# A hybrid decoder layer on one core: five first products, quartered first weights, and roots and reciprocals of norms on rows of tokens

## The chip, the cores and the metric

The kernel runs on one core of a Trainium2 chip. The engines of a core are named as in the profile: PE (matrix multiply, with PEld for its weight loads), DVE (vector), ACT (scalar functions), POOL (GpSimd) and SP, which issues most transfers. Each engine works through its own list of instructions in a fixed order. The metric is the device time of one execution in microseconds (us); lower is better.

## The reference, cut to what matters

One layer for a prompt of 1,024 tokens and 8 groups of 8 sample tokens, 1,088 in all, with 1,024 features, all in f32.

```python
def rmsnorm(x, g):
    y = x * rsqrt(mean(x * x, axis=-1, keepdims=True) + EPS)
    return y * g

xn = rmsnorm(x, norm1_g)
q, k, v, glu_a, glu_b, gate_a, gate_b = split(xn @ w_in)
branch_a = attend(q, k, v, mask, sinks) @ w_o_attn       # window 128, 16 heads, 4 kv heads
u = glu_a * sigmoid(glu_b)
c = dwconv(u)                                            # 31 taps
branch_b = silu(layernorm(c)) @ w_pb
h = x + (sigmoid(gate_a) * branch_a + sigmoid(gate_b) * branch_b) @ w_out
up = dwconv(rmsnorm(h, norm2_g) @ w_up)                  # 3 taps, 2 x 2816 channels
gate, val = split(up)
y = rmsnorm(h + (silu(gate) * val) @ w_down, norm_f_g)
```

A norm's factor belongs to a token (a column of the transposed tokens), so `xn @ w` is `(x * g) @ w` times that factor, and the factor may be applied to the product.

## The kernel before, in words

Features lie on the 128 partitions, in `KT` = 8 blocks, and tokens on the columns, in three chunks of 384, 384 and 320. Products must be as exact as f32, but PE takes fp32r operands, so each operand is split into a high part (a copy rounded to fp32r, on ACT) and a low part (the remainder, on DVE), and `mm3` makes three matmuls of each pair: high with high (L179), weight high with token low (L180), weight low with token high (L181). A product of one weight (1,024 by 128, 512 KB) with one chunk has 8 x 3 = 24 matmuls and goes into one of eight PSUM banks, four of the tag `mm` and four of the tag `aux`. `weight` loads weights two ahead through SP, and `w_split` casts them (L157, ACT) and makes the remainder (L158, DVE).

**The opening** (`phase_x`). The weights of `w_in` come in the order of `SEQUENCE`: b, a, q0, g, q0, and so on. The first four (`FIRST`) are run chunk by chunk on tokens that have been multiplied by g1 but not yet normed: `norm1_raw` makes their high and low parts (L217, L218). Meanwhile `norm1_stats` squares the tokens (L227, ACT), adds the squares of two blocks (L229, DVE) and lets PE multiply the four sums by a constant matrix 1/1024 (L233), which adds up over the partitions and gives each partition the mean square of each token. `rstd` then takes root and reciprocal of the whole 128 x 384 tile (L248 ACT, L249 DVE). The evacuations of the first four products multiply by this tile (`ev_b` L719, `ev_a` L725, `ev_q` L732, the gate L610). `norm1` then writes the normed tokens over the un-normed ones: a multiply on DVE (L242), the high part on ACT (L243), the low part half on DVE and half on POOL (L245). From the fifth weight on (the second q0), products run on normed tokens.

SP's list in the opening is: weight 0, the eight blocks of chunk 0, weights 1 and 2, chunk 1 in eight pieces, weight 3, chunk 2, then a weight at a time. ACT's own queue carries the constants, all in one transfer, ahead of a first small root that makes ACT load its table (L517). DVE derives four small constant tiles (L519 to L528) before it does anything else. PE first runs twelve matmuls on the constant matrix (L531).

**After the opening.** While PE streams the remaining products of `w_in`, attention units are woven in: scores, softmax (L265 on DVE, L270 to L272), turned by PE (L303), split into `pth` and `ptl` (`split_ps`, L196 on ACT and L197 on DVE) and multiplied with v (L315, L316). The convolution of 31 taps runs on DVE as a long list of multiply-adds (L417), which the order puts between all else.

**The end.** `ffn_down` runs the last products over three chunks of 352, 352 and 256 tokens and keeps the last 128 tokens for `tail`. For each of the three chunks `final` multiplies the sum of squares by the constant matrix (one f32 matmul, L1228), takes root and reciprocal of the whole tile (L248, L249) and scales the output in eight steps on DVE (L1232). `tail` computes the last tokens with tokens on the partitions: two products of 512 columns, their squares summed on ACT (L1252), then a short chain (L1254 to L1256) and the scaling (L1259).

The order on each engine is made ahead of time by a scheduler that follows priorities (the order of the code, moved back by `later`) and estimated costs; an edit in one place may move instructions elsewhere.

Of the kernel before, what the change touches and what calls it, by code (L numbers as in the profile page):

```python
# [45 lines left out]
FIRST = 4  # L46
# [20 lines left out]
W_SECOND = 3  # L67
W_PARTS = 2
# [8 lines left out]
def weight_order():  # L77
# [25 lines left out]
    ("ident", P),  # L103
    ("g1", KT), ("g2", KT), ("gf", KT), ("lng", KT), ("lnb", KT),
    ("cw", KT * CW), ("cb", KT), ("sink", 16), ("srow", 2), ("eps", 1),
# [10 lines left out]
class Build:  # L116
# [21 lines left out]
    def w_load(self):  # L138
        i = len(self.w_raw)
        if i < len(self.order):  # L140
            r = self.t(*(lambda p, x: (p, [P, DM], x))(*self.raw_slot(i)), bufs=2)
            self.nc.sync.dma_start(r, self.a["wall"][i])
            self.w_raw.append(r)

    def w_split(self):
        i = len(self.w_hl)
        if i < len(self.order):
            r = self.w_raw[i]
            pool, x = self.slot(i)
# [4 lines left out]
            m = W_PARTS if i < FIRST else 1  # L154
            for x in range(m):
                z = slice(x * DM // m, (x + 1) * DM // m)
                self.nc.scalar.copy(h[:, z], r[:, z])  # L157
                self.nc.vector.tensor_tensor(l[:, z], r[:, z], h[:, z].bitcast(F32), ALU.subtract)  # L158
            self.w_hl.append((h, l))
# [3 lines left out]

    def raw_slot(self, i):
        return self.wp, "wraw"
# [28 lines left out]

    def split_ps(self, h, l, src):
        self.nc.scalar.copy(h, src)  # L196
        self.nc.vector.tensor_tensor(l, src, h.bitcast(F32), ALU.subtract)  # L197
# [9 lines left out]
    def norm1_load(self, pp, c):  # L207
        o, n = CHUNKS[c]
        xr = self.t(pp, [P, KT, n], f"xr{c}")
        for k in range(KT):  # L210
            self.nc.sync.dma_start(xr[:, k, :], self.a["xT"][k, :, o:o + n])
        return xr

    def norm1_raw(self, c, xr, xh, xl):
        for k in range(KT):
            h = xh[c][:, k, :]
# [4 lines left out]
    def norm1_stats(self, pp, c, xr):  # L221
        nc = self.nc
        n = CHUNKS[c][1]
        ps = self.bank("aux")
        for k in range(KT):
            sq = self.t(pp, [P, 384], "sq", bufs=SQ_BUFS)
            nc.scalar.activation(sq[:, :n], xr[:, k, :], AF.Square)  # L227
            if k % FOLD:
                nc.vector.tensor_tensor(sq[:, :n], sq[:, :n], last[:, :n], ALU.add)  # L229
            last = sq  # L230
            if k % FOLD == FOLD - 1:
                with self.later(MEAN_LATER[c]):
                    nc.tensor.matmul(ps[:, :n], self.mean, sq[:, :n], start=k == FOLD - 1, stop=k == KT - 1)  # L233
        rstd = self.t(pp, [P, 384], f"rstd{c}")
        self.rstd(rstd[:, :n], ps[:, :n])
        return rstd

# [9 lines left out]
    def rstd(self, out, var):  # L247
        self.nc.scalar.activation(out, var, AF.Sqrt, bias=self.c("eps", 0))  # L248
# [245 lines left out]
    def run(self):  # L494
        nc, tc, a = self.nc, self.tc, self.a
        es = ExitStack()
        with es:
# [13 lines left out]
            nc.scalar.dma_start(self.consts, a["consts"])  # L511
# [7 lines left out]
            nc.vector.tensor_scalar(self.nsink, self.c("sink", 0, 16), -1.0, None, ALU.mult)  # L519
            self.cb2 = self.t(g, [P, KT], "cb2")  # L520
            nc.vector.tensor_scalar(self.cb2, self.c("cb", 0, KT), 2.0, None, ALU.mult)
            self.hsum = self.t(g, [P, KT * 16], "hsum")
            w = self.c("cw", 0, KT * CW).rearrange("p (i k) -> p i k", i=KT)
            hv = self.hsum.rearrange("p (i k) -> p i k", i=KT)
            nc.vector.tensor_tensor(hv[:, :, 0:15], w[:, :, 0:30:2], w[:, :, 1:31:2], ALU.add)
            nc.vector.tensor_copy(hv[:, :, 15:16], w[:, :, 30:31])
            self.nsrow = self.t(g, [P, 2], "nsrow")
            nc.vector.tensor_scalar(self.nsrow, self.c("srow", 0, 2), -1.0, None, ALU.mult)  # L528
# [4 lines left out]
            self.phase_x()  # L533

# [3 lines left out]
    def phase_x(self):  # L538
# [161 lines left out]
        self.slot = lambda i: (p0, "xyz"[i - 2]) if 2 <= i < FIRST else (self.wp, i % 2)  # L700
        for _ in range(W_FIRST):
            self.w_load()
        xr = [self.norm1_load(p0, 0)]
        while len(self.w_raw) < W_SECOND:
            self.w_load()
# [8 lines left out]
        def ev_b(c, o, n, ps):  # L714
            for d, x, y, r in u_part(u, o, n):
                if self.scale is None:
# [679 lines left out]
```

## Time and profile before

| | us |
|---|---|
| runs (3): median, lowest to highest | 1704.49, 1704.23 to 1704.73 |
| profiled execution | 1704.84 |
| its span, from first to last instruction | 1703.1 |
| PE busy in it | 1681.4 |
| DVE busy in it | 1287.1 |
| ACT busy in it | 848.6 |

The profile's page gives busy times of the engines, the chain of waits that ended last, and groups of equal instructions. A table of windows gives, for each stretch of time, the busy time of PE, PEld, DVE, ACT and POOL (with the number of instructions), the clock that PE was granted (1.00 is full), the busy share of the DMA engines and GB/s. A row of the timeline begins with start and duration; in brackets behind it stands how long the engine had been idle, and what it had waited for. The times are those of one execution. Matmul durations overlap: in a stream the distance between two starts tells what one costs.

### The profile page before, as it was taken

Reading aid. Unit: us, or ns where it says so; the run is one execution under the profiler, and the core shown is the slowest. Engines: PE = TensorE matmul, PEld = TensorE weight load, DVE = VectorE, ACT = ScalarE, POOL = GpSimd, SP = SyncE. Lnnn points to the kernel's source line nnn. Section 1 sums busy time; section 2 is a strip of 40 time slices with the busy share of each in tenths; the row PEclk is TensorE's granted clock in tenths of the full one; section 3 lists DMA queues with packets and bytes.
Section 4 is the critical chain, followed back from the end, with each engine's and each line's share of the span. In section 5 each row is a group of like instructions: output and inputs, shape, how many; then the busy total and the mean of one; then the engine's idle time right before and its main releaser. Section 6 shows DMA issues by size and latency. Waiting matters only on the chain.

```text
span 1703.1 us, 29147 instructions
## 1 busy us (share of the span) xinstructions
PE 1681.4 (99%) x11390; PEld 1660.6 (98%) x11390; DVE 1287.1 (76%) x2236; ACT 848.6 (50%) x1718; POOL 244.5 (14%) x430
## 2 busy tenths in 40 slices
PE   9999999999999999999999999999999999999998
PEld 8899999999999999999999999999999999999997
DVE  8999989999679986855546977777777773754437
ACT  7524477733588746973233544444444455311102
POOL 1300112130011211100000341222222220000000
PEclk9999999999999999999999999999999999999999
DMA  5112123232211265553344232222222323853103
GB/s 195 50 54 69 63 74 98 69 133 57 82 44 51 76 238 163 171 167 125 122 130 139 58 124 77 77 77 77 77 77 77 90 66 125 268 143 102 52 1 106
DMA packets 103466, 172.16 MB, mean 101 GB/s; under 512 B 44400, under 2 KB 69376, under 8 KB 103312
## 3 DMA queue, kind: packets, MB, share of 16 engines
q1 hardware_dynamic: 89760, 124.92, 24.8%
q0 software_dynamic: 13424, 45.15, 7.3%
q8 instruction: 89, 1.46, 0.4%
q14 instruction: 49, 0.40, 0.1%
q10 hardware_dynamic: 144, 0.23, 0.0%
HBM read 124.74 MB, written 47.50 MB: 101 GB/s over the span
## 4 chain that ended last, share of the span: by engine, by line
PE 89%; DVE 7%; ACT 2%; issue 1%; DMA 0%; POOL 0%; DVEq 0%; ACTq 0%; POOLq 0%
PE mm L180 22%; PE mm L181 21%; PE mm L179 21%; PE aux L181 6%; PE aux L180 6%; PE aux L179 6%; DVE c L417 2%; PE aux L303 1%; DVE bt L417 1%; PE aux L315 1%; PE aux L316 1%; PE aux L293 1%; PE aux L294 1%; ACT p L270 0%; PE aux L356 0%
## 5 line engine op out<-in xcount | busy, mean ns | idle before, releaser
L179 PE MATMUL mm<-xh,whi 128*128 128x384 f32 (+1 forms) x944 | 314.7, 333 | 0.1
L180 PE MATMUL mm<-xl,whi 128*128 128x384 f32 (+1 forms) x944 | 309.6, 328 | 3.2 <-DVE xl L245 1.7
L181 PE MATMUL mm<-xh,wlo 128*128 128x384 f32 (+1 forms) x944 | 308.8, 327 | 0.0
L180 PEld LDWEIGHTS mm<-xl,whi 128*128 128x128 f32 x944 | 178.0, 189 | 6.7 <-DVE xl L245 2.8
L179 PEld LDWEIGHTS mm<-xh,whi 128*128 128x128 f32 x944 | 178.1, 189 | 1.3 <-ACT xh L217 0.4
L181 PEld LDWEIGHTS mm<-xh,wlo 128*128 128x128 f32 x944 | 177.8, 188 | 0.1
L157 ACT CAST whi<-wraw 128x1024 fp32r<-128x1024 f32 (+1 forms) x88 | 90.4, 1030 | 175.3 <-PE aux L180 81.2
L158 DVE TENSOR_TENSOR wlo<-wraw,whi 128x1024 fp32r<-128x1024 f32 (+1 forms) x88 | 104.9, 1196 | 42.1 <-ACT whi L157 41.6
L1006 DVE SCALAR_TENSOR_TENSOR acc<-st,fc,acc 128x1104 f32<-128x1104 f32 x88 | 119.7, 1363 | 4.4 <-ACT acc L1004 3.6
L179 PE MATMUL mm<-mh,whi 128*128 128x272 f32 x368 | 106.6, 290 | 0.0
L180 PE MATMUL mm<-ml,whi 128*128 128x272 f32 x368 | 106.1, 288 | 0.0
L181 PE MATMUL mm<-mh,wlo 128*128 128x272 f32 x360 | 104.1, 289 | 0.0
L417 DVE SCALAR_TENSOR_TENSOR bt<-u,consts,bt 128x513 f32<-128x513 f32 x120 | 89.7, 747 | 0.6
L417 DVE SCALAR_TENSOR_TENSOR c<-sm,hsum,c 128x512 f32<-128x512 f32 x120 | 89.5, 746 | 0.6
L417 DVE SCALAR_TENSOR_TENSOR c<-u,consts,c 128x512 f32<-128x512 f32 x112 | 83.4, 745 | 0.5
L179 PE MATMUL mm<-gh,whi 128*128 128x384 f32 (+3 forms) x240 | 78.0, 325 | 3.4 <-ACT gh L196 3.4
L180 PE MATMUL mm<-gll,whi 128*128 128x384 f32 (+3 forms) x240 | 78.5, 327 | 0.7 <-DVE gll L197 0.7
L181 PE MATMUL mm<-gh,wlo 128*128 128x384 f32 (+3 forms) x240 | 78.7, 328 | 0.0
L180 PE MATMUL aux<-gll,whi 128*128 128x384 f32 (+3 forms) x240 | 78.2, 326 | 0.0
L179 PE MATMUL aux<-gh,whi 128*128 128x384 f32 (+3 forms) x240 | 78.2, 326 | 0.0
L181 PE MATMUL aux<-gh,wlo 128*128 128x384 f32 (+3 forms) x240 | 78.2, 326 | 0.0
L179 PE MATMUL mm<-th,whi 128*128 128x272 f32 x240 | 70.1, 292 | 2.4 <-ACT st L1128 2.2
(380 smaller groups left out, 5252.1 us busy)
## 6 DMA issues: line engine op xcount, KB each, us to landing
wraw<-wall SPq DMA_DIRECT2D x134, 512.0 KB, 4.1
d_g<-acc POOLq DMA_DIRECT2D x22, 552.0 KB, 5.2
gr<-d_g SPq DMA_DIRECT2D x20, 512.0 KB, 5.0
ga<-d_ga SPq DMA_DIRECT2D x8, 544.0 KB, 4.1
gb<-d_gb SPq DMA_DIRECT2D x8, 544.0 KB, 3.7
mar<-d_ma SPq DMA_DIRECT2D x8, 544.0 KB, 5.5
xr<-xT SPq DMA_DIRECT2D x32, 136.0 KB, 2.6
d_h<-H POOLq DMA_DIRECT2D x4, 1088.0 KB, 5.8
```

The costliest lines, as they stand in the source:

```text
L157: self.nc.scalar.copy(h[:, z], r[:, z])
L158: self.nc.vector.tensor_tensor(l[:, z], r[:, z], h[:, z].bitcast(F32), ALU.subtract)
L179: mm(ps, wh, xh, start=first, stop=False, skip_group_check=more)
L180: mm(ps, wh, xl, start=False, stop=False, skip_group_check=more)
L181: mm(ps, wl, xh, start=False, stop=last, skip_group_check=more)
L293: nc.tensor.matmul(ps[:, j, :], q[g][:, h, qs], kd[g][:, keys], start=True, stop=False)
L294: nc.tensor.matmul(ps[:, j, :], q[g][:, h, qs], kl[g][:, keys], start=False, stop=True)
L303: nc.tensor.transpose(ps[:, h * P:(h + 1) * P], pt[:, h, kb * P:(kb + 1) * P], self.ident)
L315: nc.tensor.matmul(av, v, ph, start=kb == kbs[0], stop=False)
L316: nc.tensor.matmul(av, v, pl, start=False, stop=kb == kbs[-1])
L417: mac = lambda o, x, w: nc.vector.scalar_tensor_tensor(o, x, w, o, ALU.mult, ALU.add)
L1006: nc.vector.scalar_tensor_tensor(acc, st[:, k:k + AW], fw(f, k), acc, ALU.mult, ALU.add)
```

## The change

Five things are edited.

- `FIRST` goes from 4 to 5: the second q0 product also runs on un-normed tokens and is scaled in its evacuation (`ev_q(j)`). Its split weight lies in columns of the tiles `q` that are not yet used (`spare`); the third weight is loaded into a tile of the convolution.
- The first two weights are loaded and split in quarters, between the blocks of chunk 0: SP's list is now x0, x1, a quarter of each weight, x2, x3, and so on, and only the first two quarters go through ACT's queue. For chunk 0 the first two products run side by side (`stream_side`): each block of tokens is used for both before the next. Chunks 1 and 2 come in four transfers each instead of eight.
- The constants come in two transfers, g1 and eps first; the derived tiles are made after the streams of chunk 0 (`derive`).
- `norm1_stats` adds the squares of all eight blocks on DVE, 7 adds instead of 4, and `rstd_rows` takes the place of the four mean matmuls: for each piece of at most 128 tokens (`PIECES`: 3 for 384, 4 for 320 and 352, 2 for 256) one f32 matmul with the squares as weights and one column of 1/1024, which puts the tokens on partitions (L270); a root and a reciprocal of a tile of a few columns (L287, L288); for each piece one f32 matmul that broadcasts the row with the identity (L273); and a copy on ACT (L275).
- `final` uses `rstd_rows` too.

```diff
-FIRST = 4
+FIRST = 5
...
-RAW = (0, 1, 2)
-W_FIRST = 1
-FIRST_TAGS = (("mm", "mm", "mm", "mm"), ("aux", "aux", "mm", "mm"), ("mm", "mm", "aux", "aux"))
-FOLD = 2
+FIRST_TAGS = (("mm", "mm", "mm", "mm", "aux"), ("aux", "mm", "mm", "mm", "mm"), ("aux", "mm", "mm", "mm", "mm"))
...
-W_PARTS = 2
+W_PARTS = 4
+PIECES = {384: 3, 320: 4, 352: 4, 256: 2}
...
+    def w_parts(self, m):
...
+        def part(x):
+            z = slice(x * DM // m, (x + 1) * DM // m)
+            self.nc.scalar.copy(h[:, z], r[:, z])
+            self.nc.vector.tensor_tensor(l[:, z], r[:, z], h[:, z].bitcast(F32), ALU.subtract)
+        return [lambda x=x: part(x) for x in range(m)]
...
+    def stream_side(self, xs, evacs, ws, tags, c):
+        o, n = CHUNKS[c]
+        ps = [self.bank(tag) for tag in tags]
+        for k in range(KT):
+            self.tick()
+            ks = slice(k * P, (k + 1) * P)
+            xh, xl = xs(c, k)
+            for p, (wh, wl) in zip(ps, ws):
+                self.mm3(p[:, :n], wh[:, ks], wl[:, ks], xh, xl, k == 0, k == KT - 1)
+        for p, evac in zip(ps, evacs):
+            evac(c, o, n, p)
...
+        for k in range(0, KT, 2):
+            if c == 0:
+                z = slice(k * P, (k + 2) * P)
+                for i, w in enumerate(self.w_raw):
+                    (self.nc.sync if k else self.nc.scalar).dma_start(w[:, z], self.a["wall"][i][:, z])
+                for j in (k, k + 1):
+                    self.nc.sync.dma_start(xr[:, j, :], self.a["xT"][j, :, o:o + n])
+            else:
+                self.nc.sync.dma_start(xr[:, k:k + 2, :], self.a["xT"][k:k + 2, :, o:o + n].rearrange("k p t -> p k t"))
...
-            if k % FOLD:
+            if k:
                 nc.vector.tensor_tensor(sq[:, :n], sq[:, :n], last[:, :n], ALU.add)
             last = sq
-            if k % FOLD == FOLD - 1:
-                with self.later(MEAN_LATER[c]):
-                    nc.tensor.matmul(ps[:, :n], self.mean, sq[:, :n], start=k == FOLD - 1, stop=k == KT - 1)
         rstd = self.t(pp, [P, 384], f"rstd{c}")
-        self.rstd(rstd[:, :n], ps[:, :n])
+        with self.later(MEAN_LATER[c]):
+            self.rstd_rows(pp, rstd[:, :n], last[:, :n], n)
         return rstd
+
+    def rstd_rows(self, pool, out, squares, n):
+        nc = self.nc
+        m = PIECES[n]
+        p = n // m
+        ps = self.bank("aux")
+        r = self.t(pool, [P, 4], "rows", bufs=2)
+        for j in range(m):
+            nc.tensor.matmul(ps[:p, 508 + j:509 + j], squares[:, j * p:(j + 1) * p], self.mean[:, 0:1], start=True, stop=True)
+        self.rstd(r[:p, :m], ps[:p, 508:508 + m], p)
+        for j in range(m):
+            nc.tensor.matmul(ps[:, j * p:(j + 1) * p], r[:p, j:j + 1].to_broadcast([p, P]), self.ident[:p, :p],
+                             start=True, stop=True)
+        nc.scalar.copy(out, ps[:, :n])
...
-            for w, ev, tag in zip(ws, (ev_b, ev_a, ev_q, gate_evac(*self.order[3])), FIRST_TAGS[c]):
+            evs, tags = (ev_b, ev_a, ev_q(0), gate_evac(*self.order[3]), ev_q(1)), FIRST_TAGS[c]
+            side = 0 if c else 2
+            if side:
+                self.stream_side(xs, evs[:side], ws[:side], tags[:side], c)
+            for w, ev, tag in list(zip(ws, evs, tags))[side:]:
                 self.stream(None, xs, ev, chunks=(c,), w=w, tag=tag)
-            if c and c - 1 in RAW:
+            if c == 0:
+                self.derive()
+            if c:
                 self.norm1(c - 1, xr[c - 1], rs[c - 1], xh, xl)
...
-        nc.tensor.matmul(ps[:, :n], self.mean, ssq[:, :n], start=True, stop=True)
-        self.rstd(ssq[:, :n], ps[:, :n])
+        self.rstd_rows(dt, ssq[:, :n], ssq[:, :n], n)
```

Three places of the new order matter most. The first is PE at the change from the third to the fourth product of chunk 0 (`mm_307` and `mm_338`; `whiy`, `wloy` are the fourth weight's halves, `sq_240` the sum of squares, `rows_245` the reciprocal roots). In the new order:

```order
L183 MATMUL mm_307<-xl_18_102,whix_200 128x384
L184 MATMUL mm_307<-xh_17_101,wlox_201 128x384
L270 MATMUL aux_244<-mean_76,sq_240 128x1 x3
L182 MATMUL mm_338<-xh_17_101,whiy_208 128x384
L183 MATMUL mm_338<-xl_18_102,whiy_208 128x384
L273 MATMUL aux_244<-consts_74,rows_245 128x128 x2
L184 MATMUL mm_338<-xh_17_101,wloy_209 128x384
```

and ACT's list at the same place, before and in the new order (`xh_19` is chunk 1, `xr_26` chunk 0):

```order
L227 ACTIVATE sq_233<-xr_24_126 128x384
L217 ACTIVATE xh_19_108<-xr_27_139,consts_74 128x384 x7
L157 CAST whiy_206<-wraw_148 128x512 x2
L227 ACTIVATE sq_368<-xr_27_139 128x384
L217 ACTIVATE xh_21_110<-xr_29_150,consts_74 128x320 x2
```

```order
L254 ACTIVATE sq_240<-xr_26_123 128x384
L245 ACTIVATE xh_19_103<-xr_30_145,consts_74 128x384 x7
L287 ACTIVATE rows_245<-aux_244,consts_74 128x3
L163 CAST whiy_208<-wraw_150 128x512 x2
L254 ACTIVATE sq_418<-xr_30_145 128x384
```

A small root (L287), which reads what PE's one-column matmuls (L270) make, now stands ahead of the casts of the fourth weight.

The second place is DVE where the reciprocal of chunk 1 stands, before and in the new order (`rstd_70` and `rows_443` are chunk 1's, `sq_549` to `sq_561` and `sq_637` to `sq_655` the squares of chunk 2):

```order
L245 TENSOR_TENSOR xl_18_107<-xr_24_126,xh_17_106 128x384
L229 TENSOR_TENSOR sq_549<-sq_549,sq_547 128x320
L229 TENSOR_TENSOR sq_555<-sq_555,sq_553 128x320
L249 RECIPROCAL rstd_70_392<-rstd_70_392 128x384
L229 TENSOR_TENSOR sq_561<-sq_561,sq_559 128x320
L719 TENSOR_TENSOR u_159<-aux_395,rstd_70_392 128x384
```

```order
L246 SCALAR_TENSOR_TENSOR xl_22_106<-xr_33_154,consts_74,xh_21_105 128x320 x4
L256 TENSOR_TENSOR sq_637<-sq_637,sq_635 128x320
L256 TENSOR_TENSOR sq_640<-sq_640,sq_637 128x320
L256 TENSOR_TENSOR sq_643<-sq_643,sq_640 128x320
L256 TENSOR_TENSOR sq_646<-sq_646,sq_643 128x320
L256 TENSOR_TENSOR sq_649<-sq_649,sq_646 128x320
L256 TENSOR_TENSOR sq_652<-sq_652,sq_649 128x320
L256 TENSOR_TENSOR sq_655<-sq_655,sq_652 128x320
L288 RECIPROCAL rows_443<-rows_443 128x3
L761 TENSOR_TENSOR u_159<-aux_453,rstd_73_441 128x384
```

All seven adds of chunk 2 now stand ahead of chunk 1's reciprocal, where two of four stood. On PE the broadcasting matmuls of chunk 1 stand 33 matmuls behind its one-column ones.

The third place is DVE around the first lower half of the first attention unit (`ptl`; `c` and `bt` are convolution sums). In the new order:

```order
L456 SCALAR_TENSOR_TENSOR bt_1672<-u_1492,consts_74,bt_1672 128x513
L456 SCALAR_TENSOR_TENSOR c_1670<-u_1492,consts_74,c_1670 128x512
L456 SCALAR_TENSOR_TENSOR c_1670<-sm_1671,hsum_83,c_1670 128x512
L212 TENSOR_TENSOR ptl_2104<-aux_2098,pth_2103 128x512
L456 SCALAR_TENSOR_TENSOR c_1670<-sm_1671,hsum_83,c_1670 128x512
L456 SCALAR_TENSOR_TENSOR c_1670<-u_1492,consts_74,c_1670 128x512
L361 TENSOR_TENSOR av_2129<-aux_2126,av_2129 64x512
L212 TENSOR_TENSOR ptl_2138<-aux_2132,pth_2137 128x512
```

It stands behind 97 convolution steps (L456) in the new order; before, the same `ptl` stood behind 105 (L417). At the end of the program 13 matmuls of 352 columns stand between the two groups of small matmuls of the first final norm, 6 of 256 in the second, and 3 of 512 in the third.

More of the change, by code (lines that the diff above doesn't have):

```diff
@@ L223, in norm1_stats @@
         n = CHUNKS[c][1]
-        ps = self.bank("aux")
         for k in range(KT):
@@ L510, in run @@
             self.consts = self.t(g, [P, CTOT], "consts")
-            nc.scalar.dma_start(self.consts, a["consts"])
+            first = COFF["ident"][0]
+            nc.scalar.dma_start(self.consts[:, :first], a["consts"][:, :first])
             self.ident = self.c("ident", 0, P)
@@ L1186, in down @@
             if last:
-                self.final(H, ssq, o, w)
+                self.final(dt, H, ssq, o, w)
         return ws
```

102 lines of the change are left out of this document (48 added, 54 removed).

## The prediction

> **What bounds the kernel now.** I read the page's busy times and its chain first, then the table of windows over the opening, then waits and timeline there, then the chain at the end.
>
> ```profile
> PE 1681.4 (99%) x11390; PEld 1660.6 (98%) x11390; DVE 1287.1 (76%) x2236; ACT 848.6 (50%) x1718; POOL 244.5 (14%) x430
> PE 89%; DVE 7%; ACT 2%; issue 1%; DMA 0%; POOL 0%; DVEq 0%; ACTq 0%; POOLq 0%
> ...
> 0.00:12.00 12.00, 10.48 (x48) 9.09 (x48) 6.75 (x18) 8.39 (x16) 1.13 (x9) 1.00 0.86 295
> 12.00:40.00 28.00, 28.00 (x153) 26.64 (x153) 27.11 (x46) 21.49 (x46) 3.22 (x4) 1.00 0.53 170
> 40.00:60.00 20.00, 20.00 (x123) 18.88 (x122) 16.15 (x25) 10.14 (x20) 5.73 (x6) 1.00 0.03 11
> 60.00:80.00 20.00, 17.10 (x91) 15.19 (x90) 19.85 (x29) 10.71 (x23) 8.90 (x10) 0.97 0.24 78
> 180.00:200.00 20.00, 20.00 (x148) 19.81 (x147) 19.86 (x43) 10.89 (x32) 4.32 (x8) 1.00 0.23 71
> 200.00:220.00 20.00, 18.35 (x117) 17.26 (x116) 19.66 (x44) 15.76 (x42) 3.84 (x8) 1.00 0.19 65
> 240.00:260.00 20.00, 19.95 (x131) 19.14 (x130) 13.29 (x36) 18.02 (x43) 2.31 (x8) 1.00 0.21 61
> ```
>
> PE is busy 99% of the span, so what counts is PE's own work and its few gaps. The windows (columns PE, PEld, DVE, ACT, POOL, clock, DMA) show the gaps at 0 to 12, 60 to 80 and 200 to 220 us, and a second fact: DVE, 76% over the run, is full in each window shown from 60 to 220. Time saved on PE early is kept only as far as DVE moves ahead too.
>
> **The start.** The first real product waits for supplies.
>
> ```profile
> 4.97 1.14 ACT L157 CAST whi<-wraw 128x512 fp32r<-128x512 f32 x2 [2.29 <-DMA wraw<-wall]
> 6.67 0.58 PE L179 MATMUL mm<-xh,whi 128*128 128x384 f32 x1
> 7.56 0.44 PE L180 MATMUL mm<-xl,whi 128*128 128x384 f32 x1 [0.31 <-DVE xl L218]
> ...
> 8.01 0.17 PE mm L181
> 12.17 0.77 PE aux L233 x2
> ```
>
> The whole 512 KB weight comes ahead of every token, its casts take until 6.11, and the first matmul starts at 6.67. Quarters shorten the last load and cast: I take a start at 6.0, a gain of 0.7; bounds 0 (the quarters queue behind the table load on ACT) and 1.6 (a start when the casts start). From 6.67 to 12.17 stand 24 matmuls of 0.17, 4.1 us, so 1.4 us were stalls. Two products side by side use each piece of tokens twice as long; I take half of it, 0.7, bounds 0 and 1.4. Together 1.4, of 0 to 3.0.
>
> **Norm statistics on PE.** They go from full-width to small matmuls.
>
> ```profile
> 24.70 0.65 PE aux L233 x2
> L233 PE MATMUL aux<-sq,mean 128*128 128x384 f32 x16 | 6.6, 491 | 0.0
> L233 PE MATMUL aux<-sq,mean 128*128 128x320 f32 x8 | 2.8, 430 | 0.0
> 221.50 0.84 PE aux L356 x8
> ```
>
> An f32 matmul is two instructions in the trace. Eight of 384 columns hold PE for 0.65 each; the four of 320 by columns for 0.54: 7.4 us. In their place come 3 + 3 + 4 one-column matmuls and as many broadcasting ones. The nearest row, f32 matmuls with few columns and fresh weights, has 0.84 for 8 instructions, 0.21 a matmul: 20 x 0.21 = 4.2. If one column costs its share of columns only, it is 0.06 and the sum 2.7; the upper bound is 0.33, half of the 0.65, and 6.6. I take 4.0 and a gain of 3.4, of 0.8 to 4.7.
>
> **New waits.** In the new order ACT has the small root directly ahead of the fourth weight's casts, and PE has the one-column matmuls directly ahead of that weight's product. So PE waits through a root and a half cast: 0.57 (half of 1.14) + about 0.3 (the small root of the tail, quoted below) + hand-overs: 1.0. For the second chunk DVE has seven adds of the third chunk ahead of its small reciprocal:
>
> ```profile
> L229 DVE TENSOR_TENSOR sq<-sq,sq 128x384 f32<-128x384 f32 x8 | 4.4, 544 | 0.0
> L229 DVE TENSOR_TENSOR sq<-sq,sq 128x320 f32<-128x320 f32 x4 | 1.9, 475 | 2.8 <-ACT sq L227 2.8
> L249 DVE RECIPROCAL rstd<-rstd 128x384 f32<-128x384 f32 x2 | 5.1, 2554 | 1.1 <-ACT rstd L248 1.0
> L249 DVE RECIPROCAL rstd<-rstd 128x320 f32<-128x320 f32 x1 | 2.1, 2139 | 0.0
> L732 DVE TENSOR_TENSOR qt<-mm,rstd 128x384 f32<-128x384 f32 x2 | 1.1, 548 | 0.0
> L242 DVE SCALAR_TENSOR_TENSOR xr<-xr,consts,rstd 128x384 f32<-128x384 f32 x16 | 13.0, 847 | 0.0
> ...
> 197.22 0.18 DVE den L272
> ```
>
> Seven adds are 3.3 us. The broadcasting matmuls stand 33 matmuls behind the one-column ones, 5.6 us by 0.17; root, reciprocal and hand-overs take some 0.7. By these alone nothing would wait; but DVE comes to the adds from the first chunk's norm, whose eight steps at L242 take 0.85 each, so it may be late by some microseconds. I take a wait of 1.2, of 0 to 3.3. Together 2.2, of 0.5 to 4.3.
>
> **The stall at 72 to 82 us.** PE waits there for the normed tokens of the third chunk, the first product on them being the fifth.
>
> ```profile
> 72.46 0.41 PE L180 MATMUL mm<-xl,whi 128*128 128x320 f32 x1 [1.09 <-DVE xl L245]
> ...
> 72.40:78.67 6.27, 4.40 (x21) 3.10 (x21) 6.27 (x10) 3.47 (x9) 3.79 (x4) 1.00 0.00 0
> 78.70:82.10 3.40, 3.40 (x11) 3.40 (x12) 3.27 (x7) 2.36 (x4) 3.08 (x6) 0.50 0.33 70
> 79.58 0.32 PE mm L179
> ```
>
> Matmuls of 320 columns take 0.15 (384: 0.17). From 72.40 to 78.67 PE starts 21 of them, 3.1 of 6.2 us; with the 1.09 before the first, 4.2 us are lost. Busy time does not tell it, since a matmul that trails its neighbour by 0.15 is shown 0.31 long. Behind it the granted clock is 0.50 for 3.4 us, with 0.32 between matmuls, so half of that is lost as well, 1.7. [...] With the fifth product on un-normed tokens, normed ones are needed 24 x (0.17 + 0.17 + 0.15) = 11.8 us of PE work later. DVE's work up to there: three reciprocals (7.2) become three of 0.18, nine adds more (4.7), three multiplies for the fifth product more (1.6): 0.4 less. 11.8, less the 2.6 that PE has gained by then, covers 4.2, so both losses go: 5.9; bounds 0 (DVE late with the third chunk by as much more) and 5.9.
>
> PE's account of the opening: 1.4 + 3.4 - 2.2 + 5.9 = 8.5 us.
>
> **What is late next.** The first attention unit. Its first use of a lower half (ptl) waits in DVE's row of convolution steps:
>
> ```profile
> PE aux L316 <- DVE ptl L197: 0.9, 1, 0.9
> 201.60 0.74 DVE L417 SCALAR_TENSOR_TENSOR bt<-u,consts,bt 128x513 f32<-128x513 f32 x1
> ...
> 202.93 0.68 DVE L197 TENSOR_TENSOR ptl<-aux,pth 128x512 fp32r<-128x512 f32 x1
> 203.66 0.50 PE aux L316
> ```
>
> This is DVE's own schedule, not PE's: it gets there once all ahead is done. Ahead of it the new order has 97 convolution steps instead of 105: 8 x 0.66 (two steps take from 201.60 to 202.93) = 5.3 less; with the 0.4 it is 5.7 us. Of that I take off 1.3: 1.0 for three reciprocals that stand in DVE's order while PE and ACT still make their input, about 0.3 each, and the rest for five more, smaller weight splits. That leaves 4.4, of 1.0 (the steps put off come back before the following units) to 6.5 (DVE also fills some of its 3.85 idle in 40 to 60). As 4.4 is less than PE's 8.5, DVE decides: PE arrives 8.5 early and waits 4.1 longer than now. That is what the opening is worth: 4.4 us. From 240 DVE has room (13.29 of 20), and the lead is kept.
>
> **The end.** The same small matmuls replace one full-width one in each of three final norms.
>
> ```profile
> 1660.90 0.86 PE aux L1228 x2
> 1691.12 0.45 PE aux L1228 x2
> 1692.09 1.76 DVE fssq L249
> 1693.88 3.26 DVE H L1232 x8
> 1696.49 0.19 ACT L1252 ACTIVATION_READ_ACCUMULATOR st<-mm 128x1 f32 x1
> 1697.14 0.08 DVE tsum L1254
> 1697.24 0.30 ACT tsum L1255
> ```
>
> PE is full here. For each chunk of 352: four small and four broadcasting matmuls, 8 x 0.21 = 1.7 in place of 0.86, of which some 0.2 is the filling behind a matmul of another kind, which the new ones have too: 1.0 more, twice. For 256: 0.84 for 0.45, 0.4 more. With 0.3 for a broadcast that waits, 2.7; bounds 0.7 (one column at 0.06) and 4.5 (each of the three waits 0.6 more). Something comes back: L1232 fills DVE until 1697.14, and the last sum waits for it, though ACT has its squares at 1696.68; the short reciprocal frees DVE over a microsecond sooner, so 0.3 to 0.45 is gained before ACT decides. Net 2.4 lost.
>
> **Sum.** 1704.84 (profiled execution: span 1703.1 and 1.7 around it) - 4.4 + 2.4 = 1702.8. The median of the runs is 0.35 below the profiled one: 1702.5 us.
>
> **Rivals.**
> A, DVE does not hold PE back: PE keeps 8.5. For it: ACT too is a releaser at 200, and DVE has 10.0 us idle before 60 (the first three windows). Against it: DVE's full windows from 60. 1704.5 - 8.5 + 2.4 = 1698.4.
>
> B, the grown wait at the first unit costs clock. It would be 1.65 us (PE's idle share at 200 to 220) + 4.1 of waiting within some 10 us, like the stall at 72, and then the clock halves once: 1.7 back, 1704.2. For it the row at 78.70; against it the clock column at 200 to 220, 1.00 with 1.65 us idle. [...]
>
> C, DVE paces all the way to 240: it saves in all only 0.4 of work, the steps put off are due in the next units, and the opening gives 1.0. 1704.5 - 1.0 + 2.4 = 1705.9.
>
> D, slower: the round trip costs more than the matmuls. One-column matmuls on PE, a root on ACT, a reciprocal on DVE, broadcasting matmuls on PE: each in its engine's fixed order, six times, and who comes early holds up all that is behind. If each trip holds PE or DVE up by 1.2, as I booked for the second chunk, the last three cost 3.6 in place of 0.3, and the first three take 3.6 off DVE's account in place of 1.0: 1702.5 + 3.3 + 2.6 = 1708.4. It ends over 1707.9 from 1.1 a trip on. Against it: 13 and 6 matmuls stand between the two in the first two final norms, 3 of 512 columns in the last.
>
> That the quarters start nothing earlier is no rival in time: PE's account falls to 7.1, still above DVE's 4.4.
>
> **How the numbers follow.** The forecast has 0.42, A 0.2, B 0.13, C 0.1, D 0.15. 0.2% is 3.4 us, about what can be told from no change: faster means below 1701.1, slower above 1707.9. Faster: A, and the forecast where DVE gives 6 or more, 0.12: 0.32. Slower: D, and C with the end at its upper bound (1708.0), 0.02: 0.17. Same: 0.51. The forecast alone has 1700 to 1705 (the unit's 1.0 to 6.5, the end's 0.7 to 4.5, seldom at once); the range reaches into A and D: 1697.5 to 1708.
>
> **What would show it.** Right: first product near 6; no gap and no halved clock from 72 to 82; a wait of 5 us or more at the first unit for pth and ptl; the small matmuls near 0.1 an instruction; one reciprocal of 0.18 per chunk. Wrong: a first unit without a grown wait (A), a clock of 0.5 near 200 (B), further waits for DVE until 240 (C), broadcasting matmuls in the list of waits for a microsecond each (D).

## The result, and the profile after

| | before | the change |
|---|---|---|
| median of 22 runs each, us | 1704.03 | 1706.46 |
| profiled execution, its span, us | 1704.84, 1703.1 | 1705.98, 1704.2 |

The ratio is 1.0014, interval 1.0007 to 1.0021: the change is slower by 1.2 to 3.6 us. (A second set of runs, with the experiments, gave 1705.71 against 1704.29, ratio 1.0011, 1.0002 to 1.0020.) One execution of the second set, the profiled one, took 2751 us at a granted clock of 0.56; it is in no ratio, and the row change_again below has no trace figures because of it. It is inside my bound of no change, 0.2%, and inside the range, but on the other side of where I had put it: I had forecast 2 us less.

The windows of the change over the opening (columns as before: PE, PEld, DVE, ACT, POOL, clock, DMA, GB/s):

```profile
0.00:12.00 12.00, 10.51 (x53) 10.00 (x54) 6.49 (x16) 8.09 (x17) 1.03 (x7) 1.00 0.79 239
12.00:40.00 28.00, 26.38 (x150) 24.93 (x149) 26.31 (x55) 24.29 (x52) 2.25 (x5) 1.00 0.65 213
40.00:60.00 20.00, 18.37 (x114) 18.06 (x113) 17.77 (x33) 8.33 (x18) 4.16 (x5) 1.00 0.03 11
60.00:80.00 20.00, 20.00 (x139) 20.00 (x138) 14.99 (x26) 11.14 (x22) 7.56 (x7) 1.00 0.24 78
180.00:200.00 20.00, 17.20 (x115) 16.16 (x113) 19.96 (x45) 11.81 (x34) 5.25 (x10) 1.00 0.27 80
200.00:220.00 20.00, 19.22 (x126) 18.42 (x127) 19.74 (x43) 15.13 (x39) 3.49 (x8) 1.00 0.17 65
```

PE's stall and its halved clock at 60 to 80 are gone: PE is full there, at 1.00. PE's gap at the first unit has grown (17.20 in 180 to 200). And DVE, which was full from 60 to 80 (19.85), has 5 us of idle time in that window.

**The start.** In the change's timeline:

```profile
4.08 0.62 DVE L246 SCALAR_TENSOR_TENSOR xl<-xr,consts,xh 128x384 fp32r<-128x384 f32 x1 [3.06 <-ACT xh L245]
6.40 0.45 PE L182 MATMUL mm<-xh,whi 128*128 128x384 f32 x1
7.33 0.44 PE L182 MATMUL mm<-xh,whi 128*128 128x384 f32 x1 [0.31 <-ACT whi L163]
```

Products start at 6.40 instead of 6.67, but wait more on the way: by the spacing of starts, 1.3 us were lost up to the end of the third product before (the mean matmul among them not counted), and 2.2 now. The start costs PE 0.6 instead of giving 1.4. DVE waits in pieces: for the high parts of tokens 5.0 us in four waits, of which the first is the 3.06 of this row.

**The row statistics.** The chain of waits at the fourth product, and PE's waits up to 100 us:

```profile
18.70 3.54 ACT xh L245 x7
22.24 0.15 ACT rows L287
22.39 1.03 ACT whiy L163 x2
```

```profile
21.05 0.72 PE L270 MATMUL aux<-mean,sq 128*128 128x1 f32 x6
22.95 0.44 PE L182 MATMUL mm<-xh,whiy 128*128 128x384 f32 x1 [1.17 <-DMA xr<-xT]
```

```profile
PE aux L273 <- DVE rows L288: 1.6, 1, 1.6
```

Two waits, 1.2 and 1.6, where I had 1.0 and 1.2. The bracket of the first names a load of the third chunk, which this product does not read and which lands only at 24.46, after the product has begun. The chain shows what PE waited for: seven high parts of the next chunk, then the root, then the half cast, which ends at 22.91. Three one-column matmuls, six instructions, take 0.72, and one among others holds PE for 0.22 (0.14 to the next start, whose successor follows at 0.25 instead of 0.17). In all, PE loses 10.0 us by the spacing of starts up to 169 us, 2.2 at the start and 7.8 for the statistics and their waits, where the wide matmuls took 7.4.

**DVE's idle time.** The change's waits of DVE from 40 to 100 us, then its timeline:

```profile
DVE u L761 <- ACT rstd L275: 3.5, 2, 2.0
DVE wlo L164 <- ACT whi L163: 2.9, 1, 2.9
```

```profile
66.76 1.21 DVE L164 TENSOR_TENSOR wlo<-wraw,whi 128x1024 fp32r<-128x1024 f32 x1
70.91 1.23 DVE L164 TENSOR_TENSOR wlo<-wraw,whi 128x1024 fp32r<-128x1024 f32 x1 [2.94 <-ACT whi L163]
72.05 0.17 DVE L288 RECIPROCAL rows<-rows 80x4 f32<-80x4 f32 x1
74.18 0.56 DVE L761 TENSOR_TENSOR u<-aux,rstd 128x256 f32<-128x256 f32 x2 [1.96 <-ACT rstd L275]
```

DVE waits 2.94 for a weight's high part. The tiles of this split are those of the first two weights, which PE needs until the first products of the third chunk, and these come later now that each chunk has five products. (In four_first below, with four products, the same two splits follow each other without a wait.) Behind it stands the reciprocal of the third chunk's row statistics, and behind that DVE waits 1.96 until broadcast and copy are done. Before its first lower half of the first unit DVE idles 14.9 us in the change and 11.2 before (sums of its gaps from the first instruction to that one).

**The first unit** in the change, waits and chain:

```profile
PE aux L354 <- ACT pth L211: 1.7, 1, 1.7
PE aux L342 <- ACT p L313: 1.3, 1, 1.3
PE aux L355 <- DVE ptl L212: 0.5, 1, 0.5
```

```profile
199.29 1.32 DVE c L456 x2
200.62 0.61 DVE ptl L212
201.27 0.50 PE aux L355
```

DVE reaches the lower half at 200.53 instead of 202.93 (start of the instruction; the chain gives the part that counts). PE came 4.9 us early, and its busy time shows 3.6 us of waits in 180 to 220 instead of 1.65. Behind the unit it leads the kernel before by 2.5 us from 240 on (median difference of start times of equal ACT and DVE instructions of the two traces; this is what "lead" means below). So 2.4 us of the 4.9 were lost at the unit, more than the busy times tell.

**Behind it** the lead shrinks: to 1.1 at 670 us, where a gate's load lands late, and to 0.5 at 1650. The two timelines of ACT, first before, then the change:

```profile
666.73 1.28 ACT L816 ACT_TABLE_LOAD   x1 [2.35 <-DMA ga<-d_ga]
```

```profile
665.64 1.28 ACT L855 ACT_TABLE_LOAD   x1 [3.71 <-DMA ga<-d_ga]
```

The load was issued 2.4 earlier than before (660.09 for 662.53), but took 5.5 us for 4.2.

**The end** in the change's chain:

```profile
1660.46 0.79 PE aux L270 x8
1663.41 0.64 PE aux L273 x6
1678.97 0.98 PE aux L273 x8
...
1697.58 0.70 ACT st L1289 x2
1698.30 0.17 DVE tsum L1291
```

Eight instructions, four matmuls, take 0.79, 0.20 each, as the nearest row had it. PE's last matmul starts 1.6 later than before, and the last instruction ends 1.1 later: DVE no longer holds up the last sum, ACT does.

### The profile page after: what moved, and what is told of

Read it like the earlier page. It is cut to its first block, busy times and chain, and to the rows that moved or that the text cites. A ratio compares the mean times of both kernels' runs of the same rounds, so it can differ in the third digit from the quotient of the medians.

```text
span 1704.2 us, 29288 instructions
## 1 busy us (share of the span) xinstructions
PE 1679.8 (99%) x11440; PEld 1661.6 (98%) x11440; DVE 1281.4 (75%) x2253; ACT 850.0 (50%) x1729; POOL 246.4 (14%) x430
## 4 chain that ended last, share of the span: by engine, by line
PE 83%; DVE 10%; ACT 3%; issue 2%; DMA 1%; POOL 0%; SPq 0%; DVEq 0%; ACTq 0%; POOLq 0%
PE mm L182 20%; PE mm L184 20%; PE mm L183 20%; PE aux L184 6%; PE aux L183 6%; PE aux L182 6%; DVE c L456 2%; DVE bt L456 2%; PE aux L342 1%; PE aux L354 1%; PE aux L355 1%; PE aux L332 1%; PE aux L333 1%; DMA xr<-xT 1%; DVE wlo L164 1%
## 5 line engine op out<-in xcount | busy, mean ns | idle before, releaser
L182 PE MATMUL mm<-xh,whi 128*128 128x384 f32 (+1 forms) x920 | 306.3, 333 | 0.4 <-ACT whi L163 0.3
L183 PE MATMUL mm<-xl,whi 128*128 128x384 f32 (+1 forms) x920 | 300.7, 327 | 0.2 <-DVE xl L246 0.2
L184 PE MATMUL mm<-xh,wlo 128*128 128x384 f32 (+1 forms) x920 | 300.3, 327 | 0.0
L182 PEld LDWEIGHTS mm<-xh,whi 128*128 128x128 f32 x920 | 172.9, 188 | 2.0 <-ACT whi L163 0.9
L183 PEld LDWEIGHTS mm<-xl,whi 128*128 128x128 f32 x920 | 173.0, 188 | 1.6 <-DVE xl L246 0.7
L184 PEld LDWEIGHTS mm<-xh,wlo 128*128 128x128 f32 x920 | 172.7, 188 | 0.1
L456 DVE SCALAR_TENSOR_TENSOR bt<-u,consts,bt 128x513 f32<-128x513 f32 x120 | 89.9, 750 | 0.6
L456 DVE SCALAR_TENSOR_TENSOR c<-sm,hsum,c 128x512 f32<-128x512 f32 x120 | 89.6, 747 | 0.6
L456 DVE SCALAR_TENSOR_TENSOR c<-u,consts,c 128x512 f32<-128x512 f32 x112 | 83.6, 747 | 0.2
```

Source lines behind the costliest of these rows:

```text
L182: mm(ps, wh, xh, start=first, stop=False, skip_group_check=more)
L183: mm(ps, wh, xl, start=False, stop=False, skip_group_check=more)
L184: mm(ps, wl, xh, start=False, stop=last, skip_group_check=more)
L456: mac = lambda o, x, w: nc.vector.scalar_tensor_tensor(o, x, w, o, ALU.mult, ALU.add)
```

## The experiments

Medians are of 10 or 11 runs (four_first: 5); ratios are to runs of the kernel before on the same chip, whose medians were 1703.95 to 1704.29.

| kernel | median, us | ratio, interval | PE's lead at 169 | DVE at the lower half | clock 200 to 210 | lead at 240 to 640 |
|---|---|---|---|---|---|---|
| before | 1704.0 | 1 | 0 | 202.9 | 1.00 | 0 |
| change | 1706.5 | 1.0014 (1.0007 to 1.0021) | 4.9 | 200.5 | 1.00 | 2.5 |
| less_conv_after | 1699.8 | 0.9975 (0.9966 to 0.9984) | 5.5 | 194.1 | 1.00 | 7.9 |
| old_end | 1701.3 | 0.9990 (0.9981 to 0.9999) | 5.6 | 199.9 | 1.00 | 3.1 |
| old_start | 1703.3 | 0.9996 (0.9987 to 1.0004) | 7.2 | 198.2 | 0.87 | 3.2 |
| old_stats | 1704.5 | 1.0008 (0.9999 to 1.0017) | 5.2 | 200.4 | 1.00 | 2.5 |
| change_again | 1705.7 | 1.0011 (1.0002 to 1.0020) | | | | |
| four_first | 1710.2 | 1.0034 (1.0021 to 1.0046) | 2.3 | 202.6 | 0.85 | -0.1 |
| only_five | 1701.4 | 0.9984 (0.9975 to 0.9993) | 6.0 | 199.6 | 1.00 | 3.3 |
| rows_in_opening | 1700.2 | 0.9978 (0.9969 to 0.9986) | 7.4 | 198.2 | 0.85 | 3.3 |
| end_alone | 1707.4 | 1.0020 (1.0012 to 1.0029) | 1.8 | 202.1 | 0.83 | -0.7 |
| five_and_quarters | 1702.8 | 0.9993 (0.9984 to 1.0002) | 5.1 | 200.5 | 0.83 | 0.8 |
| quarters_in_turn | 1703.1 | 0.9995 (0.9986 to 1.0004) | 5.7 | 199.9 | 0.83 | 1.5 |
| early_third | 1703.4 | 0.9996 (0.9988 to 1.0005) | 5.0 | 201.4 | 1.00 | 1.4 |

PE's lead at 169 us is taken at the same product (the 912th matmul of the streams). The lead behind the unit is not PE's lead ahead of it: it is 202.9 less DVE's time at the lower half, and 1.5 to 1.7 less where the granted clock behind it is 0.83 to 0.87 at 200 to 210. For the change that is 2.4, for early_third 1.5, for old_start and rows_in_opening 4.7 less 1.6, for five_and_quarters 2.4 less 1.7. It holds within 0.3 in all rows but two: less_conv_after (8.8 for a lead of 7.9; there PE, not DVE, comes last) and four_first (0.3 less 1.5 for -0.1). In only_five the clock is lowered ahead of the lower half, 0.83 at 190 to 200.

### Does DVE pace the first unit?

In `conv`, of the changed kernel:

```diff
         for j in range(1, 16):
+            if i < 3 and j > 9:
+                continue
             mac(bt, ev[:, j:j + half + 1], h(2 * j))
```

> The changed kernel, with 17 of 44 convolution steps left out for each of the first three convolutions (their outputs are incomplete; DVE has 16 steps, about 10.6 us, less ahead of the first attention unit). If DVE paces the first unit, PE's waits there (4.6 us in the changed kernel's profile) shrink to under 1.5, PE's lead over the kernel before stays near 4.9 us behind the unit instead of 2.4, and the time falls by 2 to 3 us against the change. Rival, the unit is paced by ACT's own work (table load and exponentials): the waits stay at 3.5 or more and the time moves by under 1 us.

Its windows:

```profile
180.00:200.00 20.00, 20.00 (x141) 19.79 (x140) 15.08 (x44) 13.04 (x39) 5.26 (x12) 1.00 0.29 91
200.00:220.00 20.00, 20.00 (x129) 19.45 (x128) 10.87 (x26) 15.59 (x38) 2.86 (x7) 1.00 0.17 61
```

PE has no gap at the unit at all, and its whole lead of 5.5 us is kept; it is 7.9 behind the unit, where the kernel before has waited. The time is 6.7 under the change's, more than expected. The step of the prediction that DVE decides there is right. The change's waits named for ACT (1.7 and 1.3) went too, though the edit takes nothing off ACT at the unit (28.6 us busy in 180 to 220, 26.9 in the change).

The second question is whether DVE's idle time or its place in the order decides. In rows_in_opening (below) the third chunk's small reciprocal is moved ahead of the two weight splits:

```diff
-MEAN_LATER = (100, 100, 100)
+MEAN_LATER = (100, 100, 30)
```

> Rows_in_opening with the third chunk's row statistics 70 steps earlier in the priorities: DVE's reciprocal for them stands ahead of two weight splits instead of behind them, and 107 convolution steps instead of 97 stand ahead of the first unit's lower half. If DVE's idle time of 4.9 us at 65 to 72 goes, but its place in the order decides at the unit, the lower half comes 6.6 - 4.9 = 1.7 later and the time is 1 to 2 over rows_in_opening's 1700.2. Rival, less idle DVE is time gained whatever the order: 1 to 3 under it.

The windows at 60 to 80 us, first of rows_in_opening, then of early_third, and the waits at early_third's unit:

```profile
60.00:80.00 20.00, 20.00 (x136) 20.00 (x135) 14.95 (x27) 10.96 (x24) 6.97 (x6) 1.00 0.26 79
```

```profile
60.00:80.00 20.00, 19.64 (x130) 19.37 (x129) 19.91 (x32) 11.52 (x25) 9.44 (x11) 1.00 0.22 44
```

```profile
PE aux L329 <- ACT p L300: 2.1, 1, 2.1
PE aux L342 <- DVE ptl L212: 1.6, 1, 1.6
PE aux L341 <- ACT pth L211: 0.7, 1, 0.7
```

DVE's 5 us of idle time are gone, and the kernel is 3.2 slower: the order fills the time with ten more convolution steps ahead of the unit, and the lower half comes 3.2 later (201.4 for 198.2). It was more than the 1.7 expected. So DVE's early idle time was worth nothing by itself; what counted is how much stands ahead of the unit in its list.

### The parts, taken out of the change one at a time

The end:

```diff
-        self.rstd_rows(dt, ssq[:, :n], ssq[:, :n], n)
+        ps = self.bank("aux")
+        nc.tensor.matmul(ps[:, :n], self.mean, ssq[:, :n], start=True, stop=True)
+        self.rstd(ssq[:, :n], ps[:, :n])
```

> The changed kernel with the final norms as before (one full-width matmul and a wide reciprocal per chunk). If the end costs what the profile shows (2.0 us on PE, 0.5 back in the last chain), the time falls by 1.5 us against the change. Rival, the small matmuls in the end are hidden or are paid back by the shorter chain: it stays within 0.5. Rival, the whole of the loss of 2.4 comes from the end: it falls by 2.4 and more and reaches the time before.

It is 5.2 under the change's first median, 4.4 under the second. That is more than the two profiles have at the end: from 1500 us to the start of the last matmul the change loses 2.7 against the kernel before and old_end gains 0.6, 3.3 together, less 0.3 for the last chain, so 3.0.

The start, as before: whole weights, one transfer of the constants, the order of loads of before, and

```diff
...
-            side = 0 if c else 2
+            side = 0
```

> The changed kernel with whole first weights, in the order of loads of before, and no products side by side (constants in one transfer). If the quarters cost time at the start, as PE's spacing suggests (first product 0.3 earlier, but 0.9 more of stalls), PE leads by some 0.6 more at 180 us; as DVE paces the first unit, the time moves by under 1 us either way. Rival, the quarters gain as I had forecast: PE's lead falls by 1.4 and the time rises by 1 or more.

2.4 to 3.2 under the change, not within 1. (The edit takes back the whole start: quarters, side by side, the constants in two transfers and the loads of the later chunks in four. "The quarters" stands for all of it below; only the side-by-side order is taken out by itself, in quarters_in_turn.) PE's lead at 169 us is 7.2 instead of 4.9, more than the 0.6 expected, and PE's wait for the second chunk's broadcast is 0.7 instead of 1.6. DVE reaches the unit's lower half 2.4 earlier, which I had not expected of a start. DVE's waits of old_start in the first 30 us, and of the change:

```profile
DVE nsink L557 <- DMA consts<-consts: 4.1, 1, 4.1
```

```profile
DVE xl L246 <- ACT xh L245: 5.0, 4, 3.1
DVE wlo L164 <- ACT whi L163: 1.0, 3, 0.6
```

The quarters make DVE wait piece by piece, 1.9 us more by these rows, and cut its splits into more instructions. Up to the lower half DVE idles 1.5 us more in the change than in old_start and is busy 0.9 us more, which makes the 2.4.

The opening's statistics, as before (four wide matmuls, wide root and reciprocal in `norm1_stats`):

```diff
...
-        with self.later(MEAN_LATER[c]):
-            self.rstd_rows(pp, rstd[:, :n], last[:, :n], n)
+        self.rstd(rstd[:, :n], ps[:, :n])
```

> The changed kernel with the opening's norms as before (four full-width matmuls and a wide root and reciprocal per chunk); the end keeps the small matmuls. If the row form costs about as much on PE as the old form (7.8 against 7.4 us with its waits), PE's lead at 180 us is 4.5 to 6 us; DVE has 0.4 us more work and fewer waits, so the first unit comes within 1 us of the change's and the time within 1 us. Rival, the row form pays as forecast: PE's lead falls by 1.2 or more and the time rises by 1 to 3.

1.3 to 2.0 under the change. PE's lead (5.2) and DVE at the unit's lower half (200.4 for 200.5) are those of the change, with 3.6 us less idle time of DVE and the wide reciprocals in their place. Both profiles end within 0.6 us of each other, so most of the difference in the times is not seen there; with intervals of 0.9 thousandths, 1.5 us, either way it is hardly resolved.

The fifth product:

```diff
-FIRST = 5
+FIRST = 4
...
```

> The changed kernel with four products on un-normed tokens instead of five (the fifth runs on normed ones again), the rest of the change kept. If only the fifth product pays for the opening, the stall near 72 us comes back (some 4 us, 6 with the clock), PE's lead at 180 us falls from 4.9 to under 1, and as DVE paces the first unit, the time rises by 1 to 3 against the change. Rival, the stall goes anyway because the reciprocals are short: no stall over 1 us, time within 1 us.

PE's waits from 30 to 100 us:

```profile
PE aux L273 <- DVE rows L288: 1.9, 2, 1.0
PE mm L183 <- POOL xl L284: 0.9, 1, 0.9
```

The stall comes back only in part (0.9 named, 1.2 by the spacing of starts), so PE leads by 2.3 at 169 us; but DVE reaches the unit hardly earlier than before, 202.6, and the clock is 0.85 from 200 to 210. The time rises by 3.7 to 4.5, more than expected. The fifth product pays at the unit, by the convolution steps that no longer stand ahead of it (106 without it, 97 with it), not by the stall alone.

### The parts, put into the kernel before

> The changed kernel unedited, on the chip of the next three. If the 5.2 us by which the old end beat it are the end's own cost, its median lies again at 1705.5 to 1707.5, 4 to 6 above the old end. Rival, the difference was mostly between two chips and two sets of runs (the two profiles differ by 1.5 to 2 at the end only): it lies at 1702.5 to 1704.5.

The change's median came back at 1705.7, within the expected band, so the change's own time is no matter of one chip; old_end ran on one chip only.

Only the fifth product (`FIRST = 5`, its spare columns, the third weight's tile, the banks and the later `derive`):

> The kernel before with the fifth product on un-normed tokens and nothing else of the change but the later derived constants and the banks. If the stall's end is the whole gain of the opening, PE leads the kernel before by 5 to 6.5 at 180 us, DVE takes half of it back at the first unit, 2 to 3.5 us are left and the time is 1700.5 to 1702. Rival, without the short reciprocals DVE has 8 us more ahead of the unit (three multiplies and the reciprocals) and nothing is left: within 0.5 of the kernel before.

2.7 us faster than the kernel before and 3.3 of lead at 240, as expected; PE's lead ahead of the unit is 6.0, the 5.9 of the stall's two terms. With the row statistics in the opening besides (the edit of old_stats, the other way round):

> The changed kernel with start and end as before: fifth product and row statistics in the opening only. If the three parts add, it is the old start's 1703.3 less what the old end gives (1.5 by the profile, up to 5 by the medians): 1698.5 to 1701.8. If the row statistics in the opening do not pay, it is not under only_five by more than 0.5; if DVE's saved reciprocals pay at the first unit, it is 1 to 2 under.

1700.2, 4 us under the kernel before (0.9969 to 0.9986) and the fastest that computes all. Against only_five PE leads by 1.4 more and DVE reaches the unit 1.4 earlier; the medians are 1.2 apart, with intervals that overlap. Without the quarters, then, the row statistics gain about what the prediction had for them on PE, 1.2; that the time gains as much is not resolved.

Quarters added to only_five, side by side and then in turn (`side` is the number of products of chunk 0 that run side by side):

```diff
...
-            side = 0
+            side = 0 if c else 2
```

> Only_five with the quartered, side-by-side start added; norms as before in the opening and the end. If the quarters cost by themselves, through DVE, which waits for pieces at the start and has more, smaller splits (2.4 us later at the first unit), it is 2 to 3 over only_five: 1703.4 to 1704.5, with DVE's first lower half of the first unit at 201 to 202.5 us against 199.6. Rival, they cost only together with the row statistics: within 0.7 of only_five.

> The same, but the two quartered products run one after the other instead of side by side. If the loads in quarters are what costs, it stays within 0.7 of five_and_quarters. If the side-by-side order costs (both weights needed at once), it is 1 or more faster; if side by side is what saves the start, it is 1 or more slower and PE's first products wait more.

1.4 and 1.7 over only_five, with intervals that overlap, and DVE 0.9 and 0.2 later at the unit: less than the 2 to 3 expected. Each lies in the other's interval, so the order side by side neither saves nor costs what could be seen. With the row statistics the quarters cost more (2.4 us at the unit and 2.4 to 3.2 of time, old_start against the change). The traces show where. With and without the row statistics, the quarters give DVE 1.5 to 1.6 us more idle time ahead of 30 us and 0.8 to 0.9 more work. Without them DVE gets 1.4 of it back, as it then waits less behind 30 us (5.0 in five_and_quarters for 6.4 in only_five); with them it gets back 0.1 (8.7 in the change for 8.9 in old_start).

The end alone, in the kernel before (the edit of old_end, the other way round):

> The kernel before with nothing changed but the final norms in the row form. If the end costs what the sum had (2.4) and the profiles show (2.3 to 2.8), it is 2.3 to 2.8 slower than the kernel before. Rival, the end costs what the medians of the change and the old end differ by: 4.4 to 5.2 slower.

3.5 slower (2.0 to 4.9). In its chain of waits:

```profile
1661.48 0.79 PE aux L255 x8
1664.44 0.86 PE aux L258 x8
```

From 1500 us to the start of the last matmul it loses 2.7 and to the last instruction 2.4, which is the first theory's number; the median lies between the two theories.

## Why the prediction was wrong

**What bounds the kernel, and that DVE decides at the first unit: right.** Shown by less_conv_after and early_third.

**The stall at 72 to 82: right on PE.** Forecast 5.9, and only_five leads by 6.0 ahead of the unit. But 1.7 of it was a halved clock (0.50 for 3.4 us) that end_alone's profile does not have: it has the same opening and the same stall, and its clock stays at 1.00 there:

```profile
60.00:80.00 20.00, 17.11 (x94) 15.18 (x94) 19.84 (x29) 10.72 (x23) 8.89 (x11) 1.00 0.24 78
78.00:83.00 5.00, 4.52 (x26) 4.52 (x27) 4.84 (x8) 3.25 (x6) 3.58 (x7) 1.00 0.27 54
```

**The step that failed: "Of that I take off 1.3 ... That leaves 4.4".** DVE's work ahead of the unit fell by 6.1 us, a little more than the 5.7 of the forecast, but its idle time rose by 3.7, not by 1.3, and it came 2.4 earlier, not 4.4. Of the 3.7, 2.8 lie behind 30 us. I had priced the three reciprocals' waits at 0.3 each and did not look at what else in DVE's list now waits for PE: the split of a weight whose tile the fifth product keeps in use (2.94), and the whole trip of the third chunk's statistics (1.96). I had the order; it shows both weight splits directly ahead of that reciprocal.

But these waits alone do not explain the missing 2.0. Rows_in_opening, with whole first weights, has them too:

```profile
DVE u L748 <- ACT rstd L262: 3.5, 2, 2.0
DVE wlo L164 <- ACT whi L163: 2.9, 1, 2.9
```

There DVE's work falls by 6.9 and its idle time rises by only 2.2, since it idles less ahead of 30 us, and it comes 4.7 earlier. So the 4.4 is what the opening gives without the quarters, by two errors of size that cancel; the quarters bring it to 2.4.

**"That the quarters start nothing earlier is no rival in time": wrong.** I let them act on PE alone, where the account had room. They act on DVE's list, which has none: 2.4 us at the unit between the change and old_start, for which the sum had no term but the 0.3 for smaller splits. The forecast gain of 1.4 at the start was a loss of 0.6.

**The row statistics in the opening: right alone, wrong beside the quarters.** I had 4.0 + 2.2 = 6.2 us in place of 7.4. Beside whole first weights they gain 1.4; in the change they take 7.8, as their waits are 2.8 instead of 2.2 and their matmuls 0.22 to 0.26.

**The end: right in its mechanism; its size is not settled.** Forecast 2.4. By the profiles it is 2.2 to 3.0 (the change and end_alone against the kernel before, the change against old_end). By the times it is more: 3.5 in end_alone (2.0 to 4.9), 4.4 to 5.2 between the medians of the change and old_end. The small matmuls cost 0.20 to 0.25, as the nearest row said (for the 0.06 of the lower bound I had no row; the change's one-column matmul among others takes 0.14 to the next start), and the gain of the last chain (0.35) came as 0.3 to 0.5. What the rest of the times is stays open.

**"The lead is kept": wrong.** 1.35 were given back at 665 us, where ACT waits for a load. The seven kernels with row statistics in the opening lost 0.2 to 1.5 there, the five without lost nothing. In rows_in_opening and only_five the load is issued at the same time, 659.29, and lands by 664.9 in the one and by 663.3 in the other. Three other transfers are issued within 4 us of it in both; where this load lands 1.6 later, the last of them on SP, a weight, lands 1.6 sooner (668.2 for 669.8). What makes the difference was not separated.

**Rival B was not weighed rightly.** Of thirteen profiles, seven have the clock at 0.83 to 0.87 over 10 us at the unit, six, the change's among them, 1.00. The mean granted clock differs between executions of one kernel: of the change's 22 runs, which spread over 6.2 us (those of before over 3.4), the eight with a mean granted clock of 0.997 have a median of 1704.6 us, the seven with 0.994 or 0.995 one of 1707.7. And the same stall can go with a lowered clock or without: the one at 72 us has 0.50 behind it in the kernel before and 1.00 in end_alone. What decides between the two was not shown. A lowered clock is not what makes the change slower in sum: its 22 runs have a mean clock of 0.9960, the 92 of the kernel before that ran beside the experiments 0.9955.

**The other rivals.** A is refuted by less_conv_after: DVE does hold PE back. C had 1705.9, the number nearest to the result, but not its mechanism: in the change PE has no named wait from 206 to 300 us, and the lead is 2.6 in 210 to 240 and 2.5 from there on. D was half right: in the opening DVE waits 3.5 us for two broadcasts, where D had 3.6 for three trips and the forecast 1.0; at the end PE has no named wait from 1650 us on.

**The sum.** In the profiled execution the lead is 2.5 at 240 us, less 2.0 given back up to 1650, less 1.6 at the end (PE's 2.0, 0.5 back): 1.1 slower, as its span has it. The medians are 2.4 and 1.4 apart. In the first set, the profiled execution of before lies 0.8 above its median and that of the change 0.5 under its own, which is the difference.

The ratios of the runs give a second account. Rows_in_opening is 3.7 us under the kernel before; old_end, which adds the quarters to it, is 1.7 under; the change, which adds the row form at the end, is 2.4 or 1.9 over. By this the opening without quarters gives 3.7 (what is lost behind it already taken off) where the forecast had 4.4, the quarters take 2.0 where it had nothing, and the end takes 3.6 to 4.1 where it had 2.4. The last two are differences of two kernels on different chips and uncertain by some 2 us each.

## What to carry to other kernels

Where a second engine paces the end of a stretch, a gain on the first is worth only what also leaves the second engine's list ahead of the place where they meet: count the instructions there, and for each of them ask what it will now wait for. Here 4.9 us of lead on PE became 2.4, which is what DVE came earlier. Cutting work into smaller pieces to start earlier can make an engine with a fixed order wait piece by piece: here DVE waited 6.0 us in seven waits of the first 30 us where, with whole weights (old_start), it waited 4.1 in one; it was the full engine, and the pieces cost more (2.4 us at the unit) than the early start brought (the first product 0.27 earlier). And a version with some of the parts can be better than one with all: here the fifth product with row statistics in the opening alone is 4 us faster than the kernel before, while the change is 2 slower.

## What was not expected of the hardware

The same stall at 72 us was followed by a granted clock of 0.50 for 3.4 us in one profile (the kernel before) and of 1.00 in another (end_alone). In the stretch ahead of the 0.50, 72.40 to 78.67, PE started 21 matmuls and was never idle for more than 1.2 us. One thing stays open: in every kernel with the row form at the end, matmuls of 384 columns in the last 190 us start 174.8 to 174.9 ns apart on average, and 174.1 in every kernel with the old end, long before the first small matmul. From 1500 to 1650 us the change loses 0.6 us of its lead without a named wait of PE, part of the end's cost.
